# The norm factor of the differential heads: logarithm and exponential on ScalarE replaced by a power on GpSimd

## The chip, the cores and the metric

The kernel runs on one core of a Trainium2 chip. The metric is the device time of one execution in microseconds (us). The core has five engines, each with an instruction queue of its own that is worked off in order: TensorE (PE; its weight loads are shown apart as PEld), VectorE (DVE), ScalarE (ACT), GpSimd (POOL) and SyncE (SP). They wait for each other through semaphores. An instruction that waits holds up everything behind it on its own engine.

## The reference, cut to what matters

The program is a stack of four layers: two hybrid layers over 528 tokens and two mixer layers over 512 tokens. The change lies in the mixer layers, in the differential attention. Each of its 8 heads subtracts two softmax maps and normalises the result over the head's 128 values:

```python
p = jax.nn.softmax(s, axis=-1)                    # two maps per head
w = p[:, 0] - lam * p[:, 1]
o_a = einsum('bhqk,bkhe->bqhe', w, v)             # 512 tokens x 8 heads x 128
o_a = o_a * rsqrt(mean(o_a * o_a, axis=-1) + EPS) * (1.0 - lam_init)
y_a = (o_a.reshape(B, S, DIFF_WIDTH) * silu(dg)) @ w_br_diff
```

The factor `rsqrt(mean + EPS)` is what the change computes in another way, 16 times in the program (8 heads, 2 layers).

## The kernel before, in words

Activations lie feature by token (128 x 512 for one head). Nearly every product of matrices is made of three: both operands are split in a rounded high part and the remainder, and high x high, high x low and low x high are added in PSUM. A projection of 128 columns over 512 tokens is therefore 24 matmuls (`dense`), first those with the high weights (tile `wh`), then 8 with the low weights (tile `wl`).

The weights come in by `weights`, line 177 on. SP loads the raw tile `wr` (512 KB, line 183). In the mixer layers ACT writes the negative into `wl` (L186), POOL issues a DMA that adds the same weights from memory onto it (L187), and ACT writes the rounded high part `wh` (L188). So POOL's queue carries one DMA issue for every chunk of weights, and a chunk's 8 last matmuls wait for that DMA. There are 3 buffers for `wr` and `wh` and 4 for `wl`.

POOL's queue also carries copies of the split keys to the other half of the partitions (L1270, L1271) and the square of each differential head's output (L1031).

The work of a head is cut in generators that are advanced between projections (`step`), so that the attention of one head is recorded among the projections of the next. A head consists of four `diff_tile` (scores of 128 queries: two matmul pairs, a masked maximum on DVE, L981, two exponentials on ACT, L1010, and the weights on DVE, L1011 to L1014) and one `diff_out` (transposes of the weights on PE, L967, their splits on ACT and DVE, L171 and L172, the product with the values, then the norm). The norm of two heads is made together, at the end of the second: `rms_rows` splits the square, sums it over the partitions with matmuls against ones, takes the logarithm (L229), and an exponential with scale -0.5 follows (L1038). Two multiplications on DVE (L1039, L1040) apply it and the gate. The result, in `ya`, is read only after all heads.

No order is written by hand beyond that. The program is recorded in this sequence, and a scheduler that plays it on a timeline of its own then sets the order in which each engine's queue gets its instructions. A changed instruction can therefore move others on every engine.

The build puts a table load ahead of an activation whose function is not in the loaded table.

Of the kernel before, what the change touches and what calls it, by code (L numbers as in the profile page):

```python
# [10 lines left out]
F32 = mybir.dt.float32  # L11
F32R = mybir.dt.float32r
AF = mybir.ActivationFunctionType
ALU = mybir.AluOpType
# [23 lines left out]
FULL = [(0, 512)]  # L38
# [15 lines left out]
def tiles4(t):  # L54
    return t.rearrange("p (i a) -> p i a", i=4)


def turned(t):

    return tiles4(t)[:, :, ::-1]  # L60


class Kernel:
# [153 lines left out]
                    with self.tc.high_priority(offset=AHEAD):  # L217
                        self.split(ps[i], vh[i // 2][:, i % 2], vl[i // 2][:, i % 2], rc[:, i : i + 1])

    def rms_rows(self, r, acc, T, halves, n, exp=True):  # L220

        nc = self.nc
        hi, lo = self.pair()
        self.split(acc[:, :T], hi[:, :T], lo[:, :T])
        for a, b in halves:
            ps = self.a()
            self.mm(ps[:, : b - a], self.ones, hi[:, a:b], True, False)
            self.mm(ps[:, : b - a], self.ones, lo[:, a:b], False, True)
            nc.scalar.activation(r[:, a:b], ps[:, : b - a], AF.Ln, bias=self.eps, scale=1.0 / n)  # L229
        if exp:  # L230
            nc.scalar.activation(r[:, :T], r[:, :T], AF.Exp, scale=-0.5)
        self.release(hi, lo)

    def norm(self, r, halves, acc, ps=None):
# [65 lines left out]
    def constants(self):  # L300
        nc, d = self.nc, self.d

        def load(name, shape):
            t = self.cp.tile(shape, F32, name=name, tag=name)
            nc.sync.dma_start(t, d[name])
            return t

        self.g0 = self.cp.tile([128, 8], F32, name="g0", tag="g0")
        nc.sync.dma_start(self.g0, d["cols"][:, COL["g", 0] : COL["g", 0] + 8])
        self.eps = self.cp.tile([128, 1], F32, name="eps", tag="eps")  # L310
        nc.vector.memset(self.eps, EPS)
        self.ones = self.cp.tile([128, 128], F32R, name="ones", tag="ones")
        nc.vector.memset(self.ones.bitcast(F32), 1.0)
        self.ones32 = self.cp.tile([128, 128], F32, name="ones32", tag="ones32")
        nc.vector.memset(self.ones32, 1.0)
        yield
        self.cols = load("cols", [128, NCOL])
        yield
        self.consts = {}
        for name, n in (("bd64", 128), ("bd4", 8), ("rot", 128), ("sel", 512)):  # L320
            t = self.slot()
            nc.sync.dma_start(t[:, :n], d[name])
            self.consts[name] = self.cp.tile([128, n], F32R, name=name + "r", tag=name + "r")
            nc.scalar.copy(self.consts[name], t[:, :n])
            self.release(t)
        reg = self.cp.tile([128, 2304], F32, name="reg1", tag="reg")
        nc.sync.dma_start(reg[:, :2080], d["tab1"])
        self.cos, self.sin = reg[:, :L1], reg[:, L1 : 2 * L1]
        self.amask = reg[:, 1056:2080].rearrange("p (a b) -> p a b", a=4)
        self.ident = load("ident", [128, 128])  # L330
        self.cmask = load("cmask", [128, 128])
        self.tri = load("tri", [128, 128])
        self.pmask = load("pmask", [128, 2, 20])


        self.v0 = self.cp.tile([128, 258], F32R, name="v0", tag="v0")
        self.w0 = self.cp.tile([128, L1], F32R, name="w0", tag="w0")
        v0 = self.v0.bitcast(F32)
        nc.gpsimd.memset(v0, 0.0)
        nc.gpsimd.memset(v0[:16, 256:257], 1.0)  # L340
        nc.gpsimd.memset(v0[64:80, 256:257], 1.0)
        nc.gpsimd.memset(self.w0.bitcast(F32), 0.0)
        self.blk = load("blk", [20, 5])
# [674 lines left out]
    def diff_out(self, hv, ws, q, k, v, gate, li, outs, ys):  # L1018

        nc = self.nc  # L1020
        yield
        self.release(q, k)
        ps = self.a()
        c = slice(128 * hv, 128 * hv + 128)
        yield from self.weighted(ps, ws, 4, lambda kt, pv: v[pv][kt // 2][:, kt % 2, c])
        self.release(ws)
        if hv:
            self.release(v)
        of, sq = self.slot(), self.slot()
        nc.scalar.copy(turned(of[:, :512]), tiles4(ps))  # L1030
        nc.gpsimd.tensor_tensor(sq[:, :512], of[:, :512], of[:, :512], ALU.mult)  # L1031
        outs.append((of, sq, gate))
        if hv:
            yield
            for _, sq, _ in outs:
                self.rms_rows(sq, sq, 512, FULL, 128, False)
            for of, sq, gate in outs:
                nc.scalar.activation(sq[:, :512], sq[:, :512], AF.Exp, scale=-0.5)  # L1038
                nc.vector.scalar_tensor_tensor(of[:, :512], of[:, :512], 0.5 * (1.0 - li), sq[:, :512], ALU.mult, ALU.mult)  # L1039
                nc.vector.tensor_tensor(of[:, :512], of[:, :512], gate[:, :512], ALU.mult)  # L1040
                self.release(sq, gate)
                ys.append(of)
# [567 lines left out]
```

## Time and profile before

| | us |
|---|---|
| median of 3 runs (2807.52 to 2809.0) | 2808.34 |
| the profiled execution | 2809.2 |
| its span, first to last instruction | 2807.4 |
| PE busy / ACT busy / DVE busy / POOL busy in it | 2752.0 / 1654.6 / 1627.0 / 689.8 |

PE is busy for 98% of the span, with the clock granted at 0.995 of full speed on average. All the time in which PE does not work is 55.4 us. The heads of the first mixer layer norm their outputs between about 1118 and 1335 us, those of the second between about 2008 and 2224 us. Times in the rows count from the span's start.

### The profile page before, as it was taken

The page shows a single profiled execution, that of the slowest core. Times are in us where ns is not written, and L with a number is a line of the kernel's source. Part 1 is how long each engine was busy: PE and PEld are TensorE (multiplying, and loading weights), DVE is VectorE, ACT ScalarE, POOL GpSimd, SP SyncE. Part 2 cuts the span into 40 slices and gives each one's busy share as a digit, 9 for nine tenths or more (in the row PEclk, how much of TensorE's full clock was granted, in tenths as well). Part 3 has the DMA queues.
Part 4 walks back from the last instruction along what each step waited for, and adds up shares of the span by engine and source line. Part 5 has one row for each costly group of instructions (what it writes and reads, how often), then busy time and mean ns, then how long its engine had stood idle before and what let it go on. Part 6 is the DMA issues. An engine that isn't in the chain of part 4 may idle for free.

```text
span 2807.4 us, 44298 instructions
## 1 busy us (share of the span) xinstructions
PE 2752.0 (98%) x16806; PEld 2439.8 (87%) x16806; DVE 1627.0 (58%) x4079; ACT 1654.6 (59%) x2926; POOL 689.8 (25%) x790
## 2 busy tenths in 40 slices
PE   8999999999999999999999999999999999999998
PEld 7999999999999878888888888888888888888886
DVE  5788784478777545665445662344676452673333
ACT  6677775677777566777555442236777664553233
POOL 4233222313322322221111211222221121211231
PEclk9999999999999999999999999999999999999999
DMA  7655657766666886756766322347765777422332
GB/s 197 142 129 128 142 133 180 188 138 133 137 142 151 198 204 160 165 126 148 167 147 163 106 76 97 107 136 185 157 150 132 156 163 160 142 78 78 103 120 68
DMA packets 137668, 395.32 MB, mean 141 GB/s; under 512 B 14031, under 2 KB 40343, under 8 KB 137327
## 3 DMA queue, kind: packets, MB, share of 16 engines
q0 software_dynamic: 39456, 143.67, 30.7%
q1 hardware_dynamic: 96846, 247.77, 26.3%
q8 instruction: 132, 2.16, 0.3%
q10 hardware_dynamic: 1152, 1.05, 0.1%
q14 instruction: 82, 0.66, 0.1%
HBM read 383.85 MB, written 8.60 MB: 140 GB/s over the span
## 4 chain that ended last, share of the span: by engine, by line
PE 88%; ACT 6%; DVE 4%; issue 1%; DMA 0%; POOL 0%; DVEq 0%; SPq 0%; ACTq 0%
PE z L165 64%; PE a L165 20%; PE a L967 1%; PE a L509 1%; ACT s L1010 1%; ACT wl L186 1%; ACT wh L188 1%; DVE s L175 1%; DVE s L981 0%; ACT L1038 0%; ACT s L174 0%; DVE s L172 0%; ACT s L171 0%; ACT L229 0%; DMA s<-mem 0%
## 5 line engine op out<-in xcount | busy, mean ns | idle before, releaser
L165 PE MATMUL z<-s,wh 128*128 128x512 f32 (+2 forms) x6784 | 1263.4, 334 | 12.3 <-DVE s L175 3.4
L165 PEld LDWEIGHTS z<-s,wh 128*128 128x128 f32 x6784 | 1042.5, 189 | 143.2 <-DVE s L175 4.6
L165 PE MATMUL z<-s,wl 128*128 128x264 f32 (+2 forms) x3392 | 660.1, 333 | 0.0
L165 PEld LDWEIGHTS z<-s,wl 128*128 128x128 f32 x3392 | 525.7, 188 | 63.1 <-issue 0.5
L187 POOL DMA_DIRECT2D wl<-w x242 | 209.7, 867 | 1060.3 <-ACT wl L186 921.4
L188 ACT CAST wh<-wr 128x1024 fp32r<-128x1024 f32 x274 | 286.7, 1046 | 309.3 <-PE z L165 304.3
L165 PE MATMUL a<-s,s 128*128 128x512 f32 (+5 forms) x1900 | 420.9, 336 | 2.7 <-ACT s L171 1.7
L186 ACT ACTIVATE wl<-wr 128x1024 fp32r<-128x1024 f32 x274 | 288.4, 1056 | 86.3 <-PE z L165 82.9
L165 PEld LDWEIGHTS a<-s,s 128*128 128x128 f32 (+1 forms) x1900 | 295.4, 186 | 33.4 <-ACT s L171 3.3
L190 ACT CAST wh<-wr 128x1024 fp32r<-128x1024 f32 x130 | 136.2, 1049 | 278.3 <-PE z L165 168.7
L192 DVE TENSOR_TENSOR wl<-wr,wh 128x1024 fp32r<-128x1024 f32 x86 | 106.9, 1244 | 199.6 <-ACT wh L190 193.9
L165 PE MATMUL z<-wh,s 128*128 128x256 f32 x1408 | 208.9, 286 | 8.0 <-DVE s L175 7.7
L192 POOL TENSOR_TENSOR wl<-wr,wh 128x1024 fp32r<-128x1024 f32 x44 | 106.3, 2416 | 441.2 <-ACT wh L190 338.6
L172 DVE TENSOR_TENSOR s<-s,s 128x512 fp32r<-128x512 f32 (+7 forms) x266 | 183.8, 704 | 44.1 <-ACT s L171 37.0
L165 PEld LDWEIGHTS z<-wh,s 128*128 128x128 f32 x1408 | 187.7, 191 | 16.5 <-DVE s L175 11.4
L172 DVE TENSOR_TENSOR s<-a,s 128x512 fp32r<-128x512 f32 (+3 forms) x266 | 150.4, 582 | 85.2 <-ACT s L171 84.0
L165 PE MATMUL a<-s,wh 128*128 128x512 f32 (+1 forms) x800 | 189.3, 384 | 0.0
L171 ACT CAST s<-s 128x512 fp32r<-128x512 f32 (+7 forms) x266 | 146.7, 565 | 70.7 <-PE a L165 15.5
L1231 DVE TENSOR_TENSOR s<-z,s 128x512 f32<-128x512 f32 x128 | 87.7, 687 | 168.3 <-PE z L165 153.0
L165 PEld LDWEIGHTS a<-s,wh 128*128 128x128 f32 x800 | 146.0, 188 | 31.9
L171 ACT CAST s<-a 128x512 fp32r<-128x512 f32 (+3 forms) x266 | 126.6, 503 | 62.2 <-PE a L967 33.7
L981 DVE CUSTOM_DVE_ANT_0 s<-a,reg 128x512 f32<-128x512 f32 x160 | 107.9, 686 | 41.2 <-PE a L165 39.6
(263 smaller groups left out, 3197.2 us busy)
## 6 DMA issues: line engine op xcount, KB each, us to landing
wr<-w SPq DMA_DIRECT2D x308, 512.0 KB, 3.5
wl<-w POOLq DMA_DIRECT2D x242, 512.0 KB, 5.9
wr<-wo SPq DMA_DIRECT2D x48, 512.0 KB, 3.6
wl<-wo POOLq DMA_DIRECT2D x32, 512.0 KB, 5.7
wr<-wb SPq DMA_DIRECT2D x32, 512.0 KB, 3.4
reg<-tab SPq DMA_DIRECT2D x24, 448.0 KB
s<-x SPq DMA_DIRECT2D x16, 264.0 KB, 7.3
r<-s SPq DMA_DIRECT2D x16, 256.0 KB, 4.5
```

The lines of the kernel that those rows point to most:

```text
L165: self.nc.tensor.matmul(out, lhsT, rhs, start=start, stop=stop)
L171: nc.scalar.copy(hi, src)
L172: nc.vector.tensor_tensor(lo, src, hi.bitcast(F32), ALU.subtract)
L175: nc.vector.scalar_tensor_tensor(lo, src, scale, hi.bitcast(F32), ALU.mult, ALU.subtract)
L186: nc.scalar.mul(lo, raw, -1.0)
L187: nc.gpsimd.dma_start(lo, src, accum_op=ALU.add)
L188: nc.scalar.copy(hi, raw)
L190: nc.scalar.copy(hi, raw)
L192: (nc.gpsimd if self.nw % 3 == 1 else nc.vector).tensor_tensor(lo, raw, hi.bitcast(F32), ALU.subtract)
L509: nc.tensor.transpose(pt[:, h], sm[h // 2][:, h % 2, 128 * c : 128 * c + 128], self.ident)
L981: self.nc.vector.tensor_tensor_reduce(e, ps, bias[:, 3 - i : 7 - i].rearrange("p a b -> p (a b)"), 1.0, LOW, ALU.add, ALU.max, mx)
L1231: nc.vector.tensor_tensor(z[:, :512], ps, r[:, :512], ALU.mult)
```

## The change

`rms_rows` becomes `mean_rows`: the sums over the partitions are the same, and ACT then writes mean + EPS (function Identity) where it wrote its logarithm. The exponential on ACT is gone. In its place POOL raises the 128 x 512 tile to the power -0.5, with a column of -0.5 broadcast as second operand. The two heads of a pair are now taken one after the other in the recording. A 128 x 1 constant is set once on DVE.

```diff
-            for _, sq, _ in outs:
-                self.rms_rows(sq, sq, 512, FULL, 128, False)
             for of, sq, gate in outs:
-                nc.scalar.activation(sq[:, :512], sq[:, :512], AF.Exp, scale=-0.5)
+                self.mean_rows(sq, sq, 512, 128)
+                nc.gpsimd.tensor_tensor(sq[:, :512], sq[:, :512], self.half.to_broadcast([128, 512]), ALU.pow)
                 nc.vector.scalar_tensor_tensor(of[:, :512], of[:, :512], 0.5 * (1.0 - li), sq[:, :512], ALU.mult, ALU.mult)
```
```diff
-    def rms_rows(self, r, acc, T, halves, n, exp=True):
+    def mean_rows(self, r, sq, T, n):
         ...
-            nc.scalar.activation(r[:, a:b], ps[:, : b - a], AF.Ln, bias=self.eps, scale=1.0 / n)
-        if exp:
-            nc.scalar.activation(r[:, :T], r[:, :T], AF.Exp, scale=-0.5)
+        self.nc.scalar.activation(r[:, :T], ps[:, :T], AF.Identity, bias=self.eps, scale=1.0 / n)
```

In the changed kernel the lines behind the edit stand 2 or 3 lower: Identity is L227, the square L1029, the power L1035, the two multiplications L1036 and L1037, the transposes L965, the key copies L1267 and L1268. Names carry numbers that are 2 higher than before (`wl_17031` is `wl_17033` now).

The scheduler moves instructions on every engine from the first norm on. ACT's queue has 48 instructions fewer: 16 exponentials and 32 table loads. POOL's has the 16 powers. Three places follow.

POOL at the norms of heads 1 and 2 of the first mixer layer, before: the square of head 2, the key copies of two later heads, and the DMAs of the next chunks.

```order
L1031 TENSOR_TENSOR s_14809<-s_14808 128x512
L1271 CAST s_14868<-s_14868 64x512
L1271 CAST s_14874<-s_14874 64x512
L187 DMA wl_15197<-w 128x1024
L187 DMA wl_15252<-w 128x1024
L1270 CAST s_15069<-s_15069 64x512
L1270 CAST s_15075<-s_15075 64x512
L1271 CAST s_15070<-s_15070 64x512
L1271 CAST s_15076<-s_15076 64x512
L187 DMA wl_15363<-w 128x1024
```

The same place on POOL now, with the powers of head 1 (`s_14514`) and head 2 (`s_14811`):

```order
L1268 CAST s_14870<-s_14870 64x512
L1035 TENSOR_TENSOR s_14514<-s_14514,half 128x512
L1268 CAST s_14876<-s_14876 64x512
L187 DMA wl_15199<-w 128x1024
L187 DMA wl_15254<-w 128x1024
L1267 CAST s_15071<-s_15071 64x512
L1267 CAST s_15077<-s_15077 64x512
L1268 CAST s_15072<-s_15072 64x512
L1268 CAST s_15078<-s_15078 64x512
L1035 TENSOR_TENSOR s_14811<-s_14811,half 128x512
L187 DMA wl_15365<-w 128x1024
```

Two DMAs, five key copies and then a third DMA now stand behind one or both powers.

POOL at the norms of heads 7 and 8 of the same layer, before:

```order
L187 DMA wl_16954<-w 128x1024
L187 DMA wl_16993<-w 128x1024
L187 DMA wl_17031<-w 128x1024
L1031 TENSOR_TENSOR s_16727<-s_16726 128x512
L187 DMA wl_17070<-w 128x1024
L187 DMA wl_17108<-w 128x1024
```

And now:

```order
L187 DMA wl_16956<-w 128x1024
L1029 TENSOR_TENSOR s_16729<-s_16728 128x512
L1029 TENSOR_TENSOR s_16508<-s_16507 128x512
L187 DMA wl_16995<-w 128x1024
L1035 TENSOR_TENSOR s_16729<-s_16729,half 128x512
L1035 TENSOR_TENSOR s_16508<-s_16508,half 128x512
L187 DMA wl_17033<-w 128x1024
L187 DMA wl_17072<-w 128x1024
L187 DMA wl_17110<-w 128x1024
```

The two powers stand one behind the other, ahead of the DMA for `wl_17033` and of those after it.

PE at the transposes of the last tile of head 8 (weights `s_16536`, made from the scores `a_16538` and `a_16542`), before. The rows are the last ones ahead of these transposes; 49 rows lie between the second scores and the first transpose.

```order
L165 MATMUL z_16735<-wh_16792,s_13807 128x256
L165 MATMUL z_16735<-wh_16792,s_13808 128x256
L165 MATMUL z_16735<-wl_16793,s_13681 128x256
L165 MATMUL z_16735<-wl_16793,s_13723 128x256
L165 MATMUL z_16735<-wl_16793,s_13765 128x256
L165 MATMUL z_16735<-wl_16793,s_13807 128x256
L967 MATMUL a_16678<-ident,s_16536 128x128
L967 MATMUL a_16687<-ident,s_16536 128x128
```

And now (weights `s_16538`, second scores `a_16544`):

```order
L165 MATMUL a_16544<-s_16173,s_16235 128x512
L165 MATMUL a_16544<-s_16174,s_16235 128x512
L965 MATMUL a_16680<-ident,s_16450 128x128
L965 MATMUL a_16680<-ident,s_16493 128x128
L965 MATMUL a_16689<-ident,s_16450 128x128
L965 MATMUL a_16689<-ident,s_16493 128x128
L965 MATMUL a_16680<-ident,s_16519 128x128
L965 MATMUL a_16689<-ident,s_16519 128x128
L965 MATMUL a_16680<-ident,s_16538 128x128
L965 MATMUL a_16689<-ident,s_16538 128x128
```

The transposes now follow the scores of the same tile after 6 other transposes.

## Rows read from the trace of the kernel before

**Rows 1.** The page, busy time of each engine (share of the span) and instructions.

```profile
PE 2752.0 (98%) x16806; PEld 2439.8 (87%) x16806; DVE 1627.0 (58%) x4079; ACT 1654.6 (59%) x2926; POOL 689.8 (25%) x790
```

**Rows 2.** Stretches: us, busy time per engine (instructions), granted clock, DMA share, GB/s.

```profile
1110.00:1210.00 100.00, 99.74 (x531) 84.44 (x530) 67.37 (x153) 77.74 (x123) 27.13 (x32) 1.00 0.64 145
1210.00:1310.00 100.00, 93.71 (x570) 82.81 (x569) 66.23 (x166) 70.62 (x129) 17.04 (x19) 0.97 0.60 140
2040.00:2140.00 100.00, 96.86 (x504) 81.83 (x503) 68.14 (x157) 69.23 (x118) 23.41 (x27) 0.98 0.61 140
2140.00:2240.00 100.00, 96.69 (x565) 83.97 (x564) 52.72 (x125) 72.26 (x114) 13.86 (x16) 1.00 0.66 146
...
1215.00:1223.50 8.50, 8.50 (x41) 7.87 (x41) 3.47 (x8) 3.81 (x6) 0.86 (x1) 0.71 0.40 104
```

**Rows 3.** Timeline of PE: start, us, work, count [idle before <-what ended it].

```profile
1211.16 0.44 PE L967 MATMUL a<-ident,s 128*128 128x128 f32 x2 [0.61 <-DVE s L1014]
1212.74 0.44 PE L967 MATMUL a<-ident,s 128*128 128x128 f32 x2 [1.14 <-DVE s L1014]
1214.53 2.08 PE L165 MATMUL z<-wh,s 128*128 128x256 f32 x8 [1.35 <-DVE s L175]
...
1277.27 0.44 PE L967 MATMUL a<-ident,s 128*128 128x128 f32 x2 [0.99 <-DVE s L1014]
1278.25 1.22 PE L165 MATMUL z<-wh,s 128*128 128x256 f32 x8 [0.54 <-DVE s L175]
```

**Rows 4.** Groups by line: busy us, mean ns of one, idle time before.

```profile
L229 ACT ACT_TABLE_LOAD x16 | 20.5, 1283 | 3.6 <-PE a L165 3.2
L1038 ACT ACT_TABLE_LOAD x16 | 20.5, 1283 | 0.3
...
L1038 ACT ACTIVATE s<-s 128x512 f32<-128x512 f32 x16 | 10.1, 632 | 0.2
```

**Rows 5.** Line L1031 alone: duration ns min/median/max, first and last start.

```profile
L1031 POOL TENSOR_TENSOR s<-s x16: 1035/1037/1401, 1092.9 to 2211.3; 128x512 f32<-128x512 f32 x16
```

**Rows 6.** The page, DMA issues: count, KB each, us from issue to landing.

```profile
wl<-w POOLq DMA_DIRECT2D x242, 512.0 KB, 5.9
```

**Rows 7.** Timeline of POOL at heads 1 and 2, and at head 7.

```profile
1121.54 1.28 POOL L1271 CAST s<-s 64x512 fp32r<-64x512 f32 x2
1122.77 0.87 POOL L187 DMA_DIRECT2D wl<-w  x1
...
1129.98 1.81 POOL L1270 CAST s<-s 64x512 fp32r<-64x512 f32 x2
1131.85 1.28 POOL L1271 CAST s<-s 64x512 fp32r<-64x512 f32 x2
...
1308.85 0.87 POOL L187 DMA_DIRECT2D wl<-w  x1 [6.45 <-ACT wl L186]
```

**Rows 8.** Timeline of PE at the first use of three chunks' low weights.

```profile
1159.07 0.39 PE L165 MATMUL z<-s,wl 128*128 128x512 f32 x1
...
1172.48 3.40 PE L165 MATMUL z<-s,wl 128*128 128x512 f32 x14
1175.72 0.38 PE L967 MATMUL a<-ident,s 128*128 128x128 f32 x2
...
1207.45 1.09 PE L165 MATMUL z<-wh,s 128*128 128x256 f32 x8
1208.38 0.40 PE L165 MATMUL z<-wl,s 128*128 128x256 f32 x2
...
1331.59 1.32 PE L165 MATMUL z<-s,wl 128*128 128x512 f32 x5
```

**Rows 9.** Timeline of ACT, the split of the weights ahead of head 3's norm.

```profile
1188.84 1.05 ACT L188 CAST wh<-wr 128x1024 fp32r<-128x1024 f32 x1 [2.91 <-PE z L165]
1190.27 0.62 ACT L171 CAST s<-s 64x512 fp32r<-64x512 f32 x1 [0.38 <-DVE s L1231]
```

**Rows 10.** Timeline of DVE, the last step of a tile's weights.

```profile
1211.93 0.75 DVE L1014 SCALAR_TENSOR_TENSOR s<-s,t,s 128x512 f32<-128x512 f32 x1
```

More of the change, by code (lines that the diff above doesn't have):

```diff
@@ L218, in dense_tok @@
                         self.split(ps[i], vh[i // 2][:, i % 2], vl[i // 2][:, i % 2], rc[:, i : i + 1])
-    def rms_rows(self, r, acc, T, halves, n, exp=True):
-        nc = self.nc
+    def mean_rows(self, r, sq, T, n):
         hi, lo = self.pair()
[L224 to L228, printed above, removed]
-            nc.scalar.activation(r[:, a:b], ps[:, : b - a], AF.Ln, bias=self.eps, scale=1.0 / n)
-        if exp:
-            nc.scalar.activation(r[:, :T], r[:, :T], AF.Exp, scale=-0.5)
+        self.split(sq[:, :T], hi[:, :T], lo[:, :T])
+        ps = self.a()
+        self.mm(ps[:, :T], self.ones, hi[:, :T], True, False)
+        self.mm(ps[:, :T], self.ones, lo[:, :T], False, True)
+        self.nc.scalar.activation(r[:, :T], ps[:, :T], AF.Identity, bias=self.eps, scale=1.0 / n)
         self.release(hi, lo)
@@ L311, in constants @@
         nc.vector.memset(self.eps, EPS)
+        self.half = self.cp.tile([128, 1], F32, name="half", tag="half")
+        nc.vector.memset(self.half, -0.5)
         self.ones = self.cp.tile([128, 128], F32R, name="ones", tag="ones")
```

## The prediction

> **What bounds the kernel now.** I read the page's busy times first: PE works for 2752.0 of 2807.4 us, ACT for 1654.6 and POOL for only 689.8 [rows 1]. PE's matmuls are the bound, so an edit on ACT or POOL can gain no more than the idle time of PE that it causes, and can lose whatever it makes PE wait. Next I read the stretches in which the heads are normed: of 400 us PE is idle for 0.26 + 6.29 + 3.14 + 3.31 = 13.0 us, and in two of them the granted clock is 0.97 and 0.98 [rows 2]. That is all that the stage has to give. [...]
>
> **What ACT loses.** 32 table loads of 1.283 us and 16 exponentials of 0.632, 41.1 + 10.1 = 51.2 us [rows 4]. Identity takes the logarithm's place and is taken to cost the same. Per head that is 3.2 us of ACT. Since PE is the bound, it counts only for PE's 13.0 idle us, and I give it nothing in the sum: the waits of PE are set anew by the new order, below.
>
> **What a power costs.** No row shows one. POOL's nearest work is the square of the same 128 x 512 tile: 1.04 us for one multiplication per element [rows 5]. That is the lower end: a power as cheap as a product. POOL has no table rows in this trace, so a power would be worked out: a logarithm (range, polynomial), a product, an exponential (range, polynomial). Some 20 multiply-adds at the price of the square are 20.8 us; 40 of them, with care for precision, 41.5, the upper end that I keep. These are estimates from the square's row. I take 20.8, because a polynomial of fewer terms does not reach single precision, and call this time P.
>
> [...]
>
> **What waits behind a power.** POOL issues the DMA that completes each chunk's low weights, and the DMAs now stand behind powers. One lands 5.9 us after its issue [rows 6]. The scheduler has moved PE work ahead of the chunks concerned, which I count in the two orders: matmuls ahead of the first use now, minus before, at 0.231 us for 512 columns (14 from 1172.48 to 1175.72), 0.118 for 256 (8 from 1207.45 to 1208.38) and 0.11 for a transpose [rows 8]. All times here are on the clock of the trace before; a delay shifts what follows it alike. One layer:
>
> - Heads 1 and 2. Power 1 starts behind a key copy, at 1121.54 + 0.6 = 1122.1 [rows 7], and ends at 1142.9. One copy (0.6), two DMAs (0.87 each) and four copies (1.81 + 1.28) follow: 1148.4. Power 2 ends at 1169.2, and the third DMA lands at 1175.1. Its weights were used from 1159.07 [rows 8]; 36 more matmuls, 7.8 us, now stand ahead: 1166.9. Late by 8.2. Of this 3.1 are waits of the next paragraph, which push the use back anyway: 5.1 us. The two DMAs behind power 1 are taken to land in time: their chunks' uses have moved back by 9.0 and 7.8 us, counted in the same way.
> - Heads 3 and 4. The square of head 4 and, behind it, its sum on PE stand behind head 3's power. ACT's Identity follows the cast at 1188.84 and ends near 1190.6 [rows 9]; power to 1211.4, square to 1212.4, cast on ACT (0.6, as such casts take there) to 1213.0. PE reaches the sum behind a chunk whose first use was at 1208.38 [rows 8], now 6.2 us of matmuls earlier, and 4.7 us of matmuls lie between: 1206.9. Late by 6.1 us. DVE meanwhile waits at L1036 for the same power, with the split of that sum and the masked maxima of the next tile queued behind; they feed the same PE rows, so this is not counted again.
> - Heads 5 and 6. Two powers run one after the other; 5.3 us of matmuls have moved ahead of the chunk behind them, and so have waits of the next paragraph. I take 0 and leave some 5 us for it in the range.
> - Heads 7 and 8. Two powers in a row, from the end of the DMA at 1308.85 + 0.87 = 1309.7 [rows 7] to 1351.3; the next DMA lands at 1357.2. Its weights were used from 1331.59 [rows 8], and 60 more matmuls, 13.0 us, now stand ahead: 1344.6. Late by 12.7 us.
>
> Together 5.1 + 6.1 + 12.7 = 23.9 a layer, 47.8 in both.
>
> **What the new order costs whatever P is.** PE's cover between a tile's last scores and its first transpose is matmul work that hides the softmax on DVE and ACT. Counted in the orders, in one layer of 32 tiles, before has 4 covers of 6 us or less (5.5, 5.8, 5.6, 6.0; mean 5.7). They are where PE waits: 0.61, 1.14, 1.35, 0.99 and 0.54, 4.6 us, or 1.16 for each [rows 3]. The changed order has 7: 5.8, 4.8, 2.5, 1.6, 2.3, 4.9 and 0.9, mean 3.3: projections that stood between scores and transposes stand elsewhere. A microsecond of missing cover is one of waiting: 7 x 1.16 + 7 x (5.7 - 3.3) = 8.1 + 17.1 = 25.2, minus the 4.6 of before: 20.6 a layer, 41.2 in both (the second layer's covers differ in one tile, 3.1 for 4.9).
>
> **The clock.** Groups of waits of 3 us or more: one a layer before; five now (the transposes of heads 3, 5 and 8, the DMAs behind the powers of heads 2 and 8). Four more at 2.2 us, two layers: 17.6.
>
> **The sum**, against the profiled execution of 2809.2: 47.8 + 41.2 + 17.6 = 106.6, and 2809.2 + 106.6 = 2915.8 us. The median of the runs lies 0.9 below that execution, so the forecast is 2915 us.
>
> **Rivals.**
>
> A. The power is short. Below 14.5 us nothing behind it is late: at heads 7 and 8 the 12.7 us fall by 2 for each microsecond of P and are gone at 20.8 - 6.35 = 14.5, at heads 3 and 4 the 6.1 at 14.7, at heads 1 and 2 the 8.2 at 16.7. The new order's covers stay short all the same: 41.2, and three groups of waits a layer instead of one, 8.8: 2858 us. For it: a product costs POOL only 1.04 us [rows 5]. Against: a power is not one step.
>
> B is the forecast, P between 14.5 and 30: 2858 to 3007.
>
> C. The power is longer than 30 us and POOL becomes the bound of the stage. Five powers a layer stand straight ahead of a wait (two, one and two), so each microsecond of P costs 10. At 41.5 us: 2915 + 10 x 20.7 = 3122. [...] Against: nothing in the trace.
>
> D. Faster. The hole at 1211 us came when ACT ran late, and 6.4 us of table loads and exponentials in the norms of heads 3 and 4 just ahead of it are gone. If the holes of the stage go with them and the new order makes none, PE gains 13.0 us and the clock 4.5: 2809.2 - 17.5 - 0.9 = 2791 us. It needs P under 14.5 and covers that suffice. It decides if the softmax, with ACT freed, gets done in the 0.9 to 2.5 us of cover that four of the tiles have left; on DVE the last step alone takes 0.75 us [rows 10], with three others and two exponentials on ACT ahead of it. The order speaks against it.
>
> E. The change does not take the table loads away. Its ACT queue shows that it does, so this has no chance of its own.
>
> **How the numbers follow.** A 0.27, B 0.48, C 0.17, D 0.05, and 0.03 for a balance of gains and waits. A measurement of this kernel can tell 0.2% (5.6 us) from no change. Faster 0.05, same 0.03, slower 0.92. The range starts below A, at 2840, for short covers that cost half, and ends at 3140, a little above C at 41.5; about 0.08 is left out below and 0.10 above.
>
> **What would show it right or wrong.** The power's row on POOL: 21 us as forecast, under 14.5 for A, over 30 for C; POOL's busy time 690 + 16 P, about 1022. ACT's busy time near 1603, without table loads at the norm. PE's waits: at the projections' low weights for POOL's DMA behind heads 2 and 8, some 5 and 13 us; at the sum of head 4 some 6; at transposes behind L1012 in more places than before. If the power takes 20 us and PE still does not wait for DMAs, the moved work was worth more than I counted. If PE's idle time in the two stages falls below 13 us, the argument on the covers is wrong.

## The result, and the profile of the changed kernel

The change makes the kernel slower by more than a third: 3859.9 us (median; 3858.0 to 3861.1) against 2807.9, a ratio of 1.3751 [1.3733, 1.3768]. The profiled execution has a span of 3859.0 us. The forecast was 2915, with an upper end of 3140.

First the page's busy times and two of its groups by line (busy us, mean ns of one, idle time before and what ended it), which answer to [rows 1, 5]:

```profile
PE 2802.0 (73%) x16806; PEld 2459.9 (64%) x16806; DVE 1643.8 (43%) x4080; ACT 1607.0 (42%) x2878; POOL 1997.1 (52%) x806
...
L1035 POOL TENSOR_TENSOR s<-s,half 128x512 f32<-128x512 f32 x16 | 1311.9, 82032 | 18.6 <-ACT s L227 17.6
L1036 DVE SCALAR_TENSOR_TENSOR s<-s,s 128x512 f32<-128x512 f32 x16 | 17.2, 1076 | 942.4 <-POOL s L1035 942.4
```

One power takes 82.0 us, 79 times the square of the same tile and four times the 20.8 us of the forecast. Sixteen of them are 1312 us, which is all of POOL's growth (689.8 to 1997.1). ACT lost 47.6 us of work; no table load of the norm is left, as the order had said [rows 4]. PE has as many instructions as before and is busy 50 us longer, and has lost its place as the bound: it is idle for 1057 us.

Then the timeline of POOL (start, us, work, count, idle time before), for heads 1 and 2 as in [rows 7], and the third power:

```profile
1119.80 0.61 POOL L1268 CAST s<-s 64x512 fp32r<-64x512 f32 x1
1120.49 81.96 POOL L1035 TENSOR_TENSOR s<-s,half 128x512 f32<-128x512 f32 x1
1202.51 1.13 POOL L1268 CAST s<-s 64x512 fp32r<-64x512 f32 x1
1203.59 1.82 POOL L187 DMA_DIRECT2D wl<-w  x2
...
1208.16 81.95 POOL L1035 TENSOR_TENSOR s<-s,half 128x512 f32<-128x512 f32 x1
1290.08 1.83 POOL L187 DMA_DIRECT2D wl<-w  x2
...
1326.07 81.94 POOL L1035 TENSOR_TENSOR s<-s,half 128x512 f32<-128x512 f32 x1 [8.05 <-ACT s L227]
```

A key copy of 1.1 us and two DMAs of 0.9 stand 82 us behind the instruction ahead of them. What that does to PE is in PE's timeline of the same layer; these are all its holes above 2.5 us from 1110 to 1900, and they answer to the three small waits of [rows 3]:

```profile
1203.70 4.08 PE L165 MATMUL a<-s,s 128*128 128x512 f32 x8 [52.20 <-POOL s L1268]
...
1294.20 1.30 PE L965 MATMUL a<-ident,s 128*128 128x128 f32 x4 [67.98 <-DVE t L979]
...
1409.73 0.80 PE L165 MATMUL a<-s,ones 128*128 128x512 f32 x1 [69.28 <-ACT s L171]
...
1503.19 3.78 PE L165 MATMUL z<-s,wl 128*128 128x512 f32 x8 [39.51 <-DMA wl<-w]
...
1683.56 1.22 PE L165 MATMUL a<-s,s 128*128 128x512 f32 x2 [120.20 <-ACT s L171]
...
1782.40 0.80 PE L165 MATMUL a<-s,s 128*128 128x256 f32 x2 [52.12 <-DVE t L979]
...
1866.74 3.71 PE L165 MATMUL z<-s,wl 128*128 128x512 f32 x8 [83.54 <-DMA wl<-w]
```

Read beside POOL's timeline, each hole ends just behind a power's end (1202.45, 1290.11 and 1408.01 for the first three). The names in the brackets differ (a key copy, DVE's masked maxima, a cast on ACT, a DMA), but POOL is behind each: the copy and the DMA are queued behind the power; the maxima at L979 are queued on DVE behind L1036, which waits for the power. The two casts differ. The one of the third hole follows a square that is queued behind a power; the one of the fifth and longest hole waited for DVE's L1036, and so for two powers in a row:

```profile
1409.06 0.62 ACT L171 CAST s<-s 128x512 fp32r<-128x512 f32 x1 [68.45 <-POOL s L1029]
...
1682.19 0.69 DVE L1036 SCALAR_TENSOR_TENSOR s<-s,s 128x512 f32<-128x512 f32 x1 [79.64 <-POOL s L1035]
...
1682.92 0.59 ACT L171 CAST s<-a 128x512 fp32r<-128x512 f32 x1 [118.94 <-DVE s L1036]
```

(That cast reads nothing that L1036 writes. Presumably it waited for the buffer of the factor, which L1036 is the last to read; the trace does not name the reason.) The seven holes are 484.8 us. The second layer has eight of this kind, 487.4 us, so together they are 972 of the 1052 us lost.

The rest is smaller waits and the clock. PE's idle time grew by 1001.6 us in all, some 29 more than these holes, and PE is busy for 50 us longer. Most of the 50 is the clock, by an estimate: half of PE's busy time at a granted clock of 0.50 is 46.4 us in this trace and was 8.4. At 0.50 eight matmuls of 128x512 behind the first and the fourth hole take 4.08 and 3.78 us, 0.47 to 0.51 each, where [rows 8] give 0.231. Three stretches (us, busy time per engine with instructions, granted clock, DMA share, GB/s), a hole and what follows two of them:

```profile
1151.00:1204.00 53.00, 0.80 (x3) 0.37 (x3) 1.48 (x2) 0.00 (x0) 52.94 (x3) 0.52 0.00 0
1204.00:1212.00 8.00, 6.69 (x32) 4.92 (x32) 6.17 (x17) 2.93 (x8) 7.69 (x7) 0.75 0.76 133
...
1294.00:1302.00 8.00, 6.29 (x15) 4.07 (x16) 5.66 (x19) 4.51 (x10) 1.36 (x2) 0.50 1.07 211
```

In the hole every engine but POOL all but stands still, and the granted clock has fallen to a mean of 0.52; in the stretches behind the first two holes it is 0.75 and 0.50. That is the loss for which the forecast took 2.2 us a group of waits.

### The profile page after: what moved, and what is told of

It is laid out like the page before. It is cut to its first block, busy times and chain, and to the rows that moved or that the text cites. A ratio compares the mean times of both kernels' runs of the same rounds, so it can differ in the third digit from the quotient of the medians.

```text
span 3859.0 us, 44265 instructions
## 1 busy us (share of the span) xinstructions
PE 2802.0 (73%) x16806; PEld 2459.9 (64%) x16806; DVE 1643.8 (43%) x4080; ACT 1607.0 (42%) x2878; POOL 1997.1 (52%) x806
## 4 chain that ended last, share of the span: by engine, by line
PE 60%; issue 20%; POOL 11%; ACT 3%; DVE 3%; DMA 2%; SPq 0%; DVEq 0%; POOLq 0%; ACTq 0%
PE z L165 43%; PE a L165 14%; POOL s L1035 11%; DMA wl<-w 2%; PE a L507 1%; PE a L965 1%; ACT wl L186 1%; DVE s L172 0%; ACT s L171 0%; ACT s L1008 0%; DMA wr<-w 0%; DVE s L979 0%; DVE s L175 0%; ACT wh L188 0%; POOL wl L187 0%
## 5 line engine op out<-in xcount | busy, mean ns | idle before, releaser
L1035 POOL TENSOR_TENSOR s<-s,half 128x512 f32<-128x512 f32 x16 | 1311.9, 82032 | 18.6 <-ACT s L227 17.6
L165 PE MATMUL z<-s,wl 128*128 128x264 f32 (+2 forms) x3392 | 671.6, 338 | 254.9 <-DMA wl<-w 254.7
L165 PE MATMUL a<-s,s 128*128 128x512 f32 (+5 forms) x1900 | 438.2, 346 | 417.9 <-ACT s L171 202.9
L186 ACT ACTIVATE wl<-wr 128x1024 fp32r<-128x1024 f32 x274 | 288.8, 1057 | 399.1 <-PE z L165 395.2
L1036 DVE SCALAR_TENSOR_TENSOR s<-s,s 128x512 f32<-128x512 f32 x16 | 17.2, 1076 | 942.4 <-POOL s L1035 942.4
L171 ACT CAST s<-s 128x512 fp32r<-128x512 f32 (+7 forms) x266 | 146.8, 566 | 335.6 <-POOL s L1029 267.7
L171 ACT CAST s<-a 128x512 fp32r<-128x512 f32 (+3 forms) x266 | 126.7, 503 | 283.7 <-DVE s L1036 194.7
L172 DVE TENSOR_TENSOR s<-s,s 128x512 fp32r<-128x512 f32 (+7 forms) x266 | 184.3, 705 | 50.4 <-ACT s L171 43.2
L172 DVE TENSOR_TENSOR s<-a,s 128x512 fp32r<-128x512 f32 (+3 forms) x266 | 150.5, 583 | 103.8 <-ACT s L171 102.4
L965 PE MATMUL a<-ident,s 128*128 128x128 f32 x448 | 78.4, 286 | 155.4 <-DVE t L979 137.3
```

The lines of the kernel that those rows point to most:

```text
L165: self.nc.tensor.matmul(out, lhsT, rhs, start=start, stop=stop)
L171: nc.scalar.copy(hi, src)
L172: nc.vector.tensor_tensor(lo, src, hi.bitcast(F32), ALU.subtract)
L186: nc.scalar.mul(lo, raw, -1.0)
L965: self.nc.tensor.transpose(pt[:, 128 * i : 128 * i + 128], es[i][:, 128 * kt : 128 * kt + 128], self.ident)
L1035: nc.gpsimd.tensor_tensor(sq[:, :512], sq[:, :512], self.half.to_broadcast([128, 512]), ALU.pow)
```

## The experiments

Two theories were to be told apart from the start. The first: the sum's structure was right, and only the length of the power was not. The second: the new order, or something that the forecast had not seen, makes a good part of the loss. The first three runs keep the changed kernel's order on every engine and shorten only the power.

**Power on 8, 128 and 256 columns, same order.** For 8 columns:

```
-nc.gpsimd.tensor_tensor(sq[:, :512], sq[:, :512], self.half.to_broadcast([128, 512]), ALU.pow)
+nc.gpsimd.tensor_tensor(sq[:, :8], sq[:, :8], self.half.to_broadcast([128, 8]), ALU.pow)
```

The price of a power in the scheduler's timeline ("the planner" here and in the expectations) is raised by 512/8 = 64, so that the plan stays the same; likewise by 4 for 128 columns and by 2 for 256. In the traces the rows of PE, ACT, POOL and SP come in the changed kernel's sequence in all three runs, and DVE's in all but 2 to 6 of 4080 places.

> The changed kernel with every engine's order unchanged, the power taken on the first 8 of 512 columns only (the other columns are scaled without it); the planner's price of a power is raised 64-fold so that it sets the same order. If a power's time goes by its columns, 82.0 us / 512 x 8 = 1.3 us. Theory 1 (the length of the powers is the loss, and the order by itself costs what the forecast gave it): the case of a short power, 2858 us. Theory 2 (the order costs nothing, only the powers do): 2808, and with the table loads gone from ACT down to 2791. Theory 3 (much of the 1052 us is the order's): above 2950.

> The same order, the power on 128 of 512 columns: about 82.0 / 4 = 20.5 us, the length that the forecast assumed. If the forecast was right in all but the size of a power: 2915 us (20.8 less 0.3 takes off some 3 us). If the loss goes straight with the power's length from nothing, 1052 / 82.0 = 12.8 us per us: 2808 + 263 = 3071. On a straight line between the short case (2858 at 14.5) and 3860 at 82.0, 14.8 us per us: 2947.

> The same order, the power on 256 of 512 columns: about 41 us, the upper end that the forecast kept. By the forecast's slope, five powers a layer in the path, 10 us per us of power: 2915 + 10 x 20.2 = 3117. If all 16 powers come into the path once they are longer than what lies between them, 16 us per us down from 3860: 3860 - 16 x 41 = 3204. Straight with the length from nothing: 2808 + 12.8 x 41 = 3333.

Measured, with one line each on L1035 (duration in ns, least/median/most; first and last start):

```profile
L1035 POOL TENSOR_TENSOR s<-s,half x16: 1636/1667/2567, 1120.7 to 2252.3; 128x8 f32<-128x8 f32 x16
```

```profile
L1035 POOL TENSOR_TENSOR s<-s,half x16: 20713/20751/21049, 1120.9 to 2322.8; 128x128 f32<-128x128 f32 x16
```

```profile
L1035 POOL TENSOR_TENSOR s<-s,half x16: 41112/41150/41447, 1121.1 to 2584.9; 128x256 f32<-128x256 f32 x16
```

| power (mean) | time, us | ratio to before | above before (2806.4) | forecast for this length |
|---|---|---|---|---|
| 1.8 us | 2863.9 | 1.0203 [1.0188, 1.0218] | 57.5 | 2858 |
| 20.8 | 2930.9 | 1.0441 [1.0426, 1.0457] | 124.4 | 2915 |
| 41.2 | 3211.8 | 1.1440 [1.1423, 1.1457] | 405.3 | 3119 |
| 82.0 (the change) | 3859.9 | 1.3751 [1.3733, 1.3768] | 1052 | none |

At the length that the forecast assumed, the time is within 16 us of it, though just as near to the 2947 of a straight line from the forecast's short case to the change. The runs at 8 and 256 columns tell the two shapes apart: a line from 1.8 us to 82.0 would give 3100 and 3353 at the two middle lengths, and both measured times lie far below it. A microsecond of power costs 3.5 us up to a length of 20.8, and much more beyond. So the first theory holds for the sum up to there (its terms are taken one by one below); the failed step is the length. The slope was wrong too: 13.8 us for each us of power between 20.8 and 41.2, and 648.1 / 40.8 = 15.9 beyond, where the forecast had 10. Sixteen is the number of powers: once one is longer than what lies between them, all come into the path, as the third expectation's 3204 had it.

**The real power under another plan.** The planner is told that a power costs what a product costs, and so sets the order that a product would get.

> The whole computation with the real power on 512 columns, but the planner takes a power at the price of a product, so the order is the one that a product in its place gets. Theory 1 (16 powers of 82 us stand in POOL's queue wherever they are put; the order hides little of them): within 3% of 3860. Rival (the order of the changed kernel had put work ahead of what waits, and without that all powers are bare): 2808 + 16 x 82 = 4120. Rival (the changed order's moved projections are a cost of their own, 41 us and its clock): 3800.

4058.2 us, ratio 1.4457 [1.4428, 1.4486]. Neither the first theory's 3860 nor the rival's 4120 is met; it lies nearer the latter. The changed kernel's order is thus 198 us the better for long powers, though with a short power it costs 57. That it hides them behind its moved matmuls is read from the orders and not shown by a run.

**A product in the power's place.** The same order as in the run before, with `ALU.mult` for `ALU.pow`.

> A product with the same constant in place of the power (1.04 us by the square's row), the order set anew by the planner for it: the norm factor is not computed, all the rest is as in the change. If freeing ACT of the table loads is worth what rival D gave: 2791 us. If ACT was never in the path: 2803 to 2812, as before. If the change's new form (norms head by head) costs what the first experiment showed whatever the planner does: about 2864. Beside the run with this very order and the real power (4058 us), the difference is what 16 powers cost in an order that was not planned for them.

2795.6 us, ratio 0.9959 [0.9946, 0.9972]: faster than before by 11.4 us. Beside 4058.2 in the same order, 16 x (82.0 - 1.04) = 1295 us of powers cost 1262.6: all but bare. Two stretches of [rows 2] in this run:

```profile
1210.00:1310.00 100.00, 98.05 (x598) 87.14 (x598) 68.49 (x163) 65.63 (x120) 19.13 (x22) 0.98 0.65 145
2040.00:2140.00 100.00, 98.18 (x527) 83.18 (x526) 68.84 (x153) 65.95 (x116) 27.31 (x31) 1.00 0.64 145
```

PE is idle for 1.95 and 1.82 us where it was for 6.29 and 3.14. So relief on ACT is worth something in this stage, two thirds of what rival D gave it at most, on two conditions: a cheap operation, and an order made for one. The short power of the first run had only the first, and lost 57 us.

**The logarithm back, with the product.** One word is changed in the run before (`AF.Identity` to `AF.Ln` in `mean_rows`).

> The product in place of the power, but Identity is the logarithm again, so ACT's table loads at the norm are back (16 logarithms, each with a load there and one on the way back: 41.1 us of ACT); the norm factor is not computed. If the 11.4 us that the product gained (2795.6) are ACT's table loads: 2804 to 2810. If they are the order that the planner finds for the head-by-head norm: 2791 to 2799.

2806.6 us, ratio 0.9993 [0.9985, 1.0002]. The gain is gone, and ACT's groups by line show what came back:

```profile
L227 ACT ACT_TABLE_LOAD x14 | 18.0, 1283 | 0.9 <-PE a L165 0.7
L1008 ACT ACT_TABLE_LOAD x12 | 15.4, 1283 | 0.2
```

These are 26 table loads; two more stand at L291, so 28 in all, 35.9 us of ACT. The logarithm itself takes as long as Identity (690 and 689 ns). The order did not change: in the two traces the rows of every engine come in the same sequence by line, operation and tile, apart from these loads. So the loads make the difference between these two runs, some 10 us by the two ratios, as the first expectation had it. With the loads in it, the new order takes as long as the kernel before.

**The price by itself.** POOL alone, three times each.

> The price by itself: GpSimd alone, nothing else of the kernel is computed. Powers of 512, 256, 128, 64, 8 and 4 columns on 128 partitions, of 512 columns on 64, 16 and 1 partitions, with three base values and four exponents, and a product beside them. The sizes run so far, 1.79 us at 8 columns, 20.83 at 128, 41.23 at 256 and 82.0 at 512, lie on 0.16 us a column and some 0.5 fixed. If a column costs the same however many partitions it has: 82 us with 1 partition too, 10.7 at 64 columns, 1.1 at 4. If the work goes by elements: 0.6 us with 1 partition. If a series is cut short by its values or exponent: other times for 1.0 or for exponent 2; a fixed program: the same to 1%.

Groups by line (busy us, mean ns of one); L1619 to L1624 are powers of fewer and fewer columns, L1627 has one partition, L1631 the exponent 2, and L1618 is the product with the same constant operand:

```profile
L1619 POOL TENSOR_TENSOR y<-x,h 128x512 f32<-128x512 f32 x3 | 245.8, 81918 | 0.2
...
L1631 POOL TENSOR_TENSOR y<-x,h 128x512 f32<-128x512 f32 x3 | 245.7, 81915 | 0.2
...
L1627 POOL TENSOR_TENSOR y<-x,h 1x512 f32<-1x512 f32 x3 | 245.7, 81905 | 0.2
L1620 POOL TENSOR_TENSOR y<-x,h 128x256 f32<-128x256 f32 x3 | 123.4, 41118 | 0.2
...
L1623 POOL TENSOR_TENSOR y<-x,h 128x8 f32<-128x8 f32 x3 | 4.9, 1636 | 0.2
L1618 POOL TENSOR_TENSOR y<-x,h 128x512 f32<-128x512 f32 x3 | 3.1, 1040 | 0.2
L1624 POOL TENSOR_TENSOR y<-x,h 128x4 f32<-128x4 f32 x3 | 3.0, 1007 | 0.2
```

A column costs (81918 - 41118) / 256 = 159.4 ns, and some 0.3 us are fixed. One partition costs as much as 128. Neither exponent nor base matters: the rows with the bases 1.0 and 3.0e-5 and the exponents 0.5 and -1 have 81915 to 81926 ns.

**The same power on 4 columns.** All rows of the tile hold the same 512 sums. The sums are taken as 128 tokens x 4 columns, and the factor is spread over the tile again:

```
-self.mean_rows(sq, sq, 512, 128)
-nc.gpsimd.tensor_tensor(sq[:, :512], sq[:, :512], self.half.to_broadcast([128, 512]), ALU.pow)
+ps = self.norm_rows(sq, 512, 128)
...
+for g in range(4):
+    for i, h in enumerate((hi, lo)):
+        self.mm(pc[:, 2 * g : 2 * g + 2], h[:, 128 * g : 128 * g + 128], self.ones[:, :2], i == 0, i == 1)
+m = sq[:, :4]
+nc.scalar.activation(m, pc[:, 0:8:2], AF.Identity, bias=self.eps, scale=1.0 / n)
+nc.gpsimd.tensor_tensor(m, m, self.half.to_broadcast([128, 4]), ALU.pow)
...
+for i, (h, r) in enumerate(((hi, mh), (lo, ml))):
+    nc.vector.tensor_tensor(t4(h), idb, r[:, :, None].bitcast(F32).to_broadcast([128, 4, 128]), ALU.mult)
+    self.mm(ps, self.ones, h[:, :T], i == 0, i == 1)
```

> The whole computation with the same power, taken where each token's sum stands once: the sums come out as 128 tokens x 4 columns, the power takes 4 columns (1.1 us by 0.16 a column), and the factor is spread to 128 x 512 again by a diagonal and two products of 512 columns with ones. If only the power's columns matter: PE gets 2 x 0.231 us more a head, 7.4 in all, and the time is 2815 us if the order costs nothing, up to 2871 with the 56 that the first experiment's order cost. If the longer chain of a head (four more steps between ACT, POOL, DVE and PE) comes into PE's path, above 2880.

2839.6 us, ratio 1.0114 [1.0097, 1.0130], between the 2815 and 2871 of the expectation: a power as the change wants it, and 1020 us faster than the change, though 1.1% slower than before. PE's busy time is 2773.0 us, 27.3 above the run with the product (2745.7). The count of 7.4 was wrong both ways. The two products that spread the factor take the place of two sums of the same width, so they add nothing: PE has 16934 matmuls, 128 more than in the run with the product. Those 128 are the narrow sums, which the count had left out and which take 15.6 us; the other 11.7 us were not taken apart.

```profile
L165 PE MATMUL a<-ones,s 128*128 128x2 f32 x128 | 15.6, 237 | 0.0
```

**Who must wait for the power?** DVE waited 942 us at L1036, so it might have been DVE that passed the loss on. In two runs nobody reads the power's result.

```
-nc.gpsimd.tensor_tensor(sq[:, :512], sq[:, :512], self.half.to_broadcast([128, 512]), ALU.pow)
+junk = self.slot()
+nc.gpsimd.tensor_tensor(junk[:, :512], sq[:, :512], self.half.to_broadcast([128, 512]), ALU.pow)
```

> The real power on 512 columns, into a tile that nobody reads: the rows are scaled by the mean itself, so DVE no longer waits for a power, and POOL's queue is as long as in the change. If what waits is mostly DVE behind its scaling (it waited 942 us there) and what stands behind that: below 2950 us. If DVE's wait is only its own part (137.3 + 105.0 us of PE's waits at splits and transposes of softmax weights): 3860 - 242 = 3618. If POOL's queue alone sets the pace (low-weight DMAs, squares and key copies behind powers): above 3750.

3844.4 us, ratio 1.3698 [1.3679, 1.3717]. This does not settle it, since among DVE's waits another has taken the place of the one removed: 475.7 us at L979, which waits for the power itself though it does not read its result, presumably for the buffers that it holds. In the next run the power touches only two constant tiles:

```
+self.tc.keep_in_program_order(nc.gpsimd.tensor_tensor(four(self.consts["sel"]),
+    self.ones32[:, None, :].to_broadcast([128, 4, 128]), self.half[:, None, :].to_broadcast([128, 4, 128]), ALU.pow))
```

> As in the run before with an unread power, but the power neither reads nor writes a buffer of the heads (a constant tile in, another out that is not used any more), held by order in POOL's queue behind what stood ahead of it; the rows are scaled by the mean itself. Nobody waits for it, for its buffer or for its result: only what stands behind it in POOL's queue does. If the queue alone makes the loss: 3650 to 3800 us (16 x 82.0 = 1312 less what PE finds to do). If the loss needs DVE to wait for the power, or for the buffers it holds (475.7 us at L979 in the run before): below 3200.

3738.3 us, ratio 1.3312 [1.3294, 1.3330]. PE's waits (us in total, times, longest):

```profile
PE z L165 <- DMA wl<-w: 735.8, 24, 59.0
PE a L165 <- POOL s L1269: 101.7, 2, 50.8
```

Here nobody waits for the power, and 930 us are lost all the same: DMAs and key copies behind it in POOL's queue suffice. In the change itself these two are 302.8 and 104.5 us, because other waits on the same powers end later there:

```profile
PE a L165 <- ACT s L171: 341.5, 15, 120.2
PE z L165 <- DMA wl<-w: 302.8, 12, 83.6
PE a L965 <- DVE t L979: 137.3, 4, 68.2
PE a L165 <- DVE t L979: 105.0, 4, 52.2
PE a L165 <- POOL s L1268: 104.5, 2, 52.3
```

Three of the seven holes above end through DVE's L1036 (68.0, 120.2 and 52.1 us), but to free DVE alone gave back only the 122 us between the two runs. How much of them is DVE's share is left open, since the order differs too.

**Newton's iteration on POOL.** Each step is

```
+nc.gpsimd.tensor_tensor(t, y, y, ALU.mult)
+nc.gpsimd.tensor_tensor(t, t, x, ALU.mult)
+nc.gpsimd.tensor_scalar(t, t, -0.5, 1.5, ALU.mult, ALU.add)
+nc.gpsimd.tensor_tensor(y, y, t, ALU.mult)
```

> The whole computation, the factor by three steps of Newton's iteration: two integer instructions on DVE for a first guess, then 12 products on POOL at 1.04 us, 12.5 us a head instead of 82.0, and no table loads. By the forecast's rule (below 14.5 us on POOL nothing behind is late): the time is set by the order, between 2796 (as with the product) and 2864 (as in the first experiment). If a head's longer chain is bare in PE: 16 x 12.5 = 200 us more, 2996.

2868.5 us, ratio 1.0216 [1.0202, 1.0230]: 4.5 us above the upper end of what was expected. The four lines take longer than the square did:

```profile
L252 POOL TENSOR_TENSOR s<-s,s 128x512 f32<-128x512 f32 x48 | 69.9, 1457 | 1.4
L254 POOL TENSOR_TENSOR s<-s,s 128x512 f32<-128x512 f32 x48 | 69.9, 1457 | 1.8
L251 POOL TENSOR_TENSOR s<-s 128x512 f32<-128x512 f32 x48 | 58.2, 1212 | 30.7 <-DVE s L249 25.3 <-DVE t L1021 4.0
L253 POOL TENSOR_SCALAR s<-s 128x512 f32<-128x512 f32 x48 | 38.8, 808 | 1.3
```

Together they are 3 x 4.93 = 14.8 us a head, not 12.5, just above the 14.5 from which the forecast expected lateness. But of PE's waits only little is for low weights:

```profile
PE a L977 <- DVE s L1024: 32.7, 13, 6.0
PE z L165 <- DVE s L175: 26.3, 12, 8.3
...
PE z L165 <- DMA wl<-w: 2.6, 2, 2.1
```

The first line are transposes that wait for the softmax, whose last step is on DVE. DVE itself is slower in this run. It is busy for 1746.7 us, against 1635.9 in the run with the product, and its 32 new instructions are only 17.3 of that. Two of its lines: the last step of the softmax weights (busy us, mean ns), and a subtraction in the split of the queries (ns least/median/most; first and last start):

```profile
L1024 DVE SCALAR_TENSOR_TENSOR s<-s,t,s 128x512 f32<-128x512 f32 x64 | 63.8, 997 | 1.6
...
L1291 DVE TENSOR_TENSOR s<-s,s x32: 684/687/9335, 1032.6 to 2201.9; 64x512 fp32r<-64x512 f32 x32
```

The last step takes 747 ns in the run with the product. The subtraction takes 0.69 us in most places and 9.3 us in two, each beside an unbroken row of Newton's instructions on POOL; PE's two waits of 8.3 us at L175 end just behind them. So at least a part of the loss is DVE's longer instructions beside POOL's products, and next to nothing is late low weights. What the new order adds is not shown.

**Before, with one more table instruction.**

```
+nc.scalar.preload_act_table_set("natural_log_exp_and_others")
 nc.scalar.activation(r[:, a:b], ps[:, : b - a], AF.Ln, bias=self.eps, scale=1.0 / n)
```

> The kernel before with its own formulas; one instruction more ahead of each head's logarithm, which loads a table that holds logarithm and exponential. It reads and writes no tile, so the planner puts it far ahead, and the 32 table loads of the norms stay: all that changes in the heads is the order of the other instructions. If the order is what the stage's time hangs on (PE waits in the heads and the clock behind them, 17.5 us by the forecast's count, and some of the 55.4 us that PE is idle in all): 2780 to 2795 us. If table loads are what counts: 2804 to 2810.

2803.6 us, ratio 0.9986 [0.9978, 0.9995]: it beats both kernels, by some 4 us over before, and misses the 2780 to 2795 that were expected of a better order. PE is idle for 12.9 us in the four stretches of [rows 2], as before (13.0), so the gain lies elsewhere, and why is not shown.

## Why the prediction was wrong, point by point

- **The bound, and what ACT loses.** Right. ACT fell to 1607.0 us (forecast 1603), without table loads at the norm. Whether giving this nothing in the sum was right for this order no run shows; with a cheap operation and its own order it would have been 11.4 us, nearly all of it the table loads.
- **The length of a power: the step that failed.** "Some 20 multiply-adds at the price of the square" made 20.8 us, and 41.5 was kept as the upper end. It is 82.0, twice that end. The number of steps was a guess from how a power could be worked out, and nothing in the trace limited it from above; the range took the guess's end for a bound. With 82.0 in place of 20.8 the forecast's own slope gives 2915 + 10 x 61.2 = 3527 us; the other 333 us are the slope's, below.
- **What waits behind a power of 20.8 us.** Right in place and, within 2 us, in size. At that length the timeline of PE has, in one layer, these waits behind powers at heads 2, 4 and 8:

```profile
1180.43 3.78 PE L165 MATMUL z<-s,wl 128*128 128x512 f32 x8 [5.05 <-DMA wl<-w]
...
1229.01 0.80 PE L165 MATMUL a<-s,ones 128*128 128x512 f32 x1 [8.09 <-ACT s L171]
...
1401.46 3.78 PE L165 MATMUL z<-s,wl 128*128 128x512 f32 x8 [12.74 <-DMA wl<-w]
```

  against 5.1, 6.1 and 12.7 forecast, by the counts from [rows 5 to 9]. In the second layer they are 4.94, 6.80 and 12.78.
- **The new order's covers and the clock.** 41.2 and, for a short power, 8.8 us of clock were forecast, 50.0 together; the run with 8 columns measured 57.5. In its profile PE is idle for 86.9 us (55.4 before) and busy for 22.3 more. So the waits, 31.5 us more, were put too high. The clock was near: a granted mean of 0.991 over 2861.2 us, against 0.995 over 2807.4, loses some 26 us against 14, so 12 more, a part of them while PE was idle. The rest of the 22.3 was not taken apart. The 2.2 us for a group of waits, from which the 8.8 here and the 17.6 of the sum are made, was set between 0.29 x 8.5 = 2.5 and 0.02 x 100 = 2.0 from [rows 2]; no run shows such a price for a group. Where the 17.6 was forecast, at a power of 20.8 us, the run with 128 columns has a granted mean of 0.981 over 2928.9 us: by the same estimate some 42 us more than before, again a part of them while PE was idle. The place was right only in part. PE's waits at the transposes, before and with 8 columns:

```profile
PE a L967 <- DVE s L1014: 5.8, 7, 1.1
```

```profile
PE a L965 <- DVE s L1012: 15.1, 13, 1.8
```

  These are 9.3 of the 31.5 us. They came in more places, as forecast, but the longest is 1.8 us and the mean 1.16: the 2.4 us that each short cover was to add did not come there (34.2 us of the sum in both layers). Much of the rest is waits at splits, which the covers do not count: behind ACT's L171 11.5 us where it was 4.0, behind DVE's L172 5.6 where it was 1.2. That 50.0 came near 57.5 is in part luck.
- **The slope of rival C.** Too small, the second mis-sized term: 10 us for each us of power, where 13.8 and 15.9 were measured. It counted five powers a layer that stand straight ahead of a wait at 20.8 us and held it for every length. Heads 5 and 6, taken at 0, make 120.2 us at 82.0; the key copy behind power 1 and the maxima behind L1036, both named, got no time of their own and end 52.2 and 68.0 us of waits. Covers of some 20 us a power run out, and then every power counts: (3859.9 - 2863.9) / 16 = 62 us of each 82 are bare.
- **Rival D.** Its price, 17.5 us at most (13.0 of PE's idle time and 4.5 of clock, the 2.5 and 2.0 above), was of the right size: 11.4 were measured under its two conditions. In the changed kernel neither held.
- **The other marks.** The formula 690 + 16 P for POOL's busy time gives 2002 for 82.0; the page has 1997.1. The first power starts at 1120.5, forecast 1122.1.

## What to carry to other kernels

An operation that no row shows has no upper bound from rows: run it by itself first, or leave the range open to several times the guess, and work out the slope for a length at which every cover is used up, not only the first ones. An engine with 25% load is not spare for long instructions if it also issues the DMAs and copies that the bound engine waits for: ask what stands behind each of them in its queue. A scheduler's order made for a long operation costs by itself (57 us here with the power cut to 1.8), so the price of an operation and the order that it brings are measured apart, as with the short power in the same order.

## What the runs showed of the hardware

A power on POOL costs 159.4 ns a column, the same for 1 partition and for 128, and for every base and exponent tried: 79 times a product of the same shape (1040 ns). A product of two different tiles on POOL took 1457 ns in the kernel with Newton's iteration, of a tile with itself 1212, and 1039 where POOL ran alone; what makes the difference was not taken apart. Beside those products one subtraction of two tiles on DVE took 9.3 us, twice, where 0.69 is its median. Beside the long powers it did not: 16 of the same subtractions ran wholly inside powers of the changed kernel, in 684 to 689 ns each.
